# All eleven feature pairs of both SwiGLU blocks by Strassen's scheme, with three pairs' upper left quarter first

## The chip, the cores and the metric

The kernel runs on one core of one Trainium2 chip. The metric is the device time of one execution in microseconds (us). The kernel before takes 1882.31 us, the median of three runs (1882.1 to 1882.53). PE is TensorE (matrix products and transposes), DVE is VectorE, ACT is ScalarE, POOL is GpSimd, SP is SyncE, which only issues DMAs here.

## The reference, cut to what matters

One decoder layer on 1024 rows (S) of width 1024 (D): a half weighted SwiGLU, a mixing block of attention, and a second half weighted SwiGLU.

```python
def _rms(x, g):
    y = x * rsqrt(mean(x * x, axis=-1) + EPS)
    return y * g

def _swiglu(x, g, w_gate, w_up, w_down):
    h = _rms(x, g)
    return (silu(h @ w_gate) * (h @ w_up)) @ w_down

x = x + 0.5 * _swiglu(x, ffn1_norm, ffn1_w_gate, ffn1_w_up, ffn1_w_down)
h = _rms(x, mix_norm)
...                       # dilated attention and latent attention on h, giving o
x = x + o @ w_out
x = x + 0.5 * _swiglu(x, ffn2_norm, ffn2_w_gate, ffn2_w_up, ffn2_w_down)
```

The hidden width of both SwiGLUs is 2816, or 22 feature tiles of 128. The change is in the first half of a SwiGLU alone, `h @ w_gate` and `h @ w_up`, and in both SwiGLUs alike.

## The kernel before, in words

**Products.** A float32 operand is split into a rounded high part and the low rest, and a product is the sum of three matmuls, high by high (L120), high by low (L121) and low by high (L122). A matmul takes 128 contraction rows and writes 512 columns of a PSUM bank. `split` (L97) makes the parts of an operand: ACT copies the high part (L99), then DVE subtracts it from the operand to give the low part (L100).

**The two halves of h.** `ffn` (L218) normalizes the eight row tiles (`norm_rows`: squares on ACT at L186 and DVE at L183, a chain of three small steps on POOL that ends at L131, scaling on DVE at L193) into `y[0]` to `y[7]`. `bank` (L226) transposes four row tiles at one of eight column tiles into a PSUM bank. `Block.put` copies a bank out, times the gain, as a high part (ACT, L212) and a low part (DVE, L213). So h stands transposed as four Blocks of four column tiles each: B11 and B21 are rows 0 to 511 (first and second half of D), B12 and B22 are rows 512 to 1023, which need `y[4]` to `y[7]`.

**Strassen's scheme.** A pair of feature tiles, two halves of D and two halves of the rows make a product of two by two blocks. Done plainly it takes 8 block products, by Strassen's scheme (in Winograd's form) 7. One block product is four column tiles by three matmuls, 12 matmuls: a pair takes 96 per weight matrix plainly and 84 by the scheme. The scheme works on four sums of h's Blocks, T1 to T4 (`sums`, L242 to L259: T1 is B12 less B11, T2 is B22 less T1, T3 is B22 less B12, T4 is B21 less T2; made by POOL, L235 and L255, and DVE, L246, L250 and L251), and on four sums of each weight pair, S1 to S4 (`make`, L285, sums on POOL at L295). The seven products of a weight matrix are named by their weight operand: M11 with B11 and M12 with B21 give the upper left result C11 (`start`, which adds two banks, L517); S1 with T1, S3 with T3 and S2 with T2 go on from M11's bank (`middle`, L522 to L530); S4 with B22 and M22 with T4 end it (`close`, L532). `finish` (L330) multiplies the activated gate by the up result, stores the four quarters of a pair, and makes the four sums that the down projection needs, two on DVE (L347, L348) and two on POOL (L349, L350), each pair of them with a DMA behind it.

**The order of the work.** Pair 0 is done plainly: `half_unit` (L322) makes 24 matmuls for one feature tile and one row half, 8 of them in all. Feature 0's row half 0 comes first, since it needs only `y[0]` to `y[3]`; the transposes of the second row half stand behind its second unit, and the eight half units stretch over the time in which T1 to T4 are made. Pairs 1 to 10 then go by the scheme, with gate and up products interleaved; `AHEAD` products ahead the weights' sums and splits are issued (`prepare`). The loads of a weight matrix's two tiles are issued when M11 of the matrix before it is prepared. Behind pair 10 stands the down projection (L467 to L475), which is also by the scheme.

The queues are in order: each engine executes its instructions as they stand in the program, and an instruction that waits holds up all that stand behind it on that engine. A scheduler sets how the instructions of the code are interleaved per engine.

**What stands ahead of each SwiGLU.** The first one begins with loads of x from HBM: rows 0 to 3, the first tile of both weights, rows 4 to 7, the second tile of both. Ahead of the second one stands the output projection of the mixing block, a row tile at a time (`out_rows`, 24 matmuls, ended by a DVE addition at L1212); behind each row tile come its norm and the write of the tile to `x2` in HBM (POOL, L1287). All eight are done before the second SwiGLU begins.

Of the kernel before, what the change touches and what calls it, by code (L numbers as in the profile page):

```python
# [10 lines left out]
F32 = mybir.dt.float32  # L11
# [7 lines left out]
P = 128  # L19
# [28 lines left out]
EARLYH = 4  # L48
ESTEPS = 5
# [10 lines left out]
def tile_layer(ctx: ExitStack, tc: tile.TileContext, x, g1n, mixn, g2n, wg1, wu1, wd1, wg2, wu2, wd2,  # L60
# [157 lines left out]
    def ffn(rows_in, ys, gain, wg, wu, wd, act_d, xsrc, done, aside=iter(())):  # L218
# [10 lines left out]
        B11, B12, B21, B22, T1, T2, T3, T4 = (Block() for _ in range(8))  # L229

        def whole(blk, k, eng):

            d = tmp([P, 512])
            hi, lo = blk.hi_lo(k)
            eng.tensor_tensor(d, hi.bitcast(F32), lo.bitcast(F32), op=ALU.add)  # L235
            return d

        def turned(blk, th, k):
            kf = k + 4 * (blk in (B21, B22))
            blk.put(k, bank(th, kf), gcol[:, kf:kf + 1])  # L240

        def sums():  # L242
            for k in range(4):
                b12 = whole(B12, k, nc.gpsimd)
                t1 = whole(B11, k, nc.vector)
                nc.vector.tensor_tensor(t1, b12, t1, op=ALU.subtract)  # L246
                T1.put(k, t1)
                yield
                t3 = whole(B22, k, nc.gpsimd)
                nc.vector.tensor_tensor(t1, t3, t1, op=ALU.subtract)  # L250
                nc.vector.tensor_tensor(t3, t3, b12, op=ALU.subtract)  # L251
                T3.put(k, t3)
                yield
                t4 = whole(B21, k, nc.gpsimd)
                nc.gpsimd.tensor_tensor(t4, t4, t1, op=ALU.subtract)  # L255
                T2.put(k, t1)
                yield
                T4.put(k, t4)
                yield  # L259
# [7 lines left out]
        order = []  # L267
        PAIRS = range(1, NF // 2)
        for c in PAIRS:
            order += [(c, "g", w) for w in ("M11", "M12")]  # L270
            if c > 1:
                order += [(c - 1, "u", w) for w in ("S4", "M22")]
            order += [(c, "g", w) for w in ("S1", "S3", "S2")]
            order += [(c, "u", w) for w in ("M11", "M12")]
            order += [(c, "g", w) for w in ("S4", "M22")]
            order += [(c, "u", w) for w in ("S1", "S3", "S2")]
        order += [(NF // 2 - 1, "u", w) for w in ("S4", "M22")]
        raws, sums_, ready = {}, {}, {}
        made = [0]

        def load_pair(c, nme):
            if c < NF // 2:
                raws[(c, nme)] = [raw_of((wg if nme == "g" else wu)[2 * c + j]) for j in range(2)]
# [1087 lines left out]
```

## Time and profile before

| what | us |
|---|---|
| median of three runs | 1882.31 |
| the profiled execution's own time | 1881.59 |
| its span (first to last instruction) | 1879.8 |
| PE busy | 1825.7 |
| DVE busy | 1271.2 |
| ACT busy | 775.4 |
| POOL busy | 627.8 |
| first SwiGLU: PE's first transposes, and its last wait before a long stretch without waits | 7.08 and 84.00 |
| second SwiGLU's first transposes | 1221.56 |

The profile is of one execution. Its rows are of this kind: an engine, the line of the kernel, the operation, the tiles it writes and reads, how many instructions of a kind follow each other, and in brackets the idle time of the engine just before and what ended it. Matmuls are pipelined, so that the span of one (0.39 us) is longer than the distance from one to the next. The granted TensorE clock (PEclk) was 0.993 of full speed over the whole span. Outside the span lie 1881.59 - 1879.8 = 1.8 us.

### The profile page before, as it was taken

The page shows a single profiled execution, that of the slowest core. Times are in us where ns is not written, and L with a number is a line of the kernel's source. Part 1 is how long each engine was busy: PE and PEld are TensorE (multiplying, and loading weights), DVE is VectorE, ACT ScalarE, POOL GpSimd, SP SyncE. Part 2 cuts the span into 40 slices and gives each one's busy share as a digit, 9 for nine tenths or more (in the row PEclk, how much of TensorE's full clock was granted, in tenths as well). Part 3 has the DMA queues.
Part 4 walks back from the last instruction along what each step waited for, and adds up shares of the span by engine and source line. Part 5 has one row for each costly group of instructions (what it writes and reads, how often), then busy time and mean ns, then how long its engine had stood idle before and what let it go on. Part 6 is the DMA issues. An engine that isn't in the chain of part 4 may idle for free.

```text
span 1879.8 us, 25149 instructions
## 1 busy us (share of the span) xinstructions
PE 1825.7 (97%) x9088; PEld 1546.2 (82%) x9088; DVE 1271.2 (68%) x2127; ACT 775.4 (41%) x1782; POOL 627.8 (33%) x706
## 2 busy tenths in 40 slices
PE   7899999999999999999998999979999999999998
PEld 5688888888888888888998888868888888888887
DVE  7976766766968363337888683388676767678681
ACT  5333333334445242236876582243333333253550
POOL 5643455442000122332454521256445444510000
PEclk9899999999999999999999999989999999999999
DMA  4223243326943231123311232313224222397422
GB/s 179 79 90 109 95 142 122 102 78 244 343 140 107 96 128 34 34 69 112 91 37 29 57 114 78 124 56 107 96 84 135 96 99 92 105 337 269 123 62 90
DMA packets 87078, 215.50 MB, mean 115 GB/s; under 512 B 11847, under 2 KB 17689, under 8 KB 86953
## 3 DMA queue, kind: packets, MB, share of 16 engines
q1 hardware_dynamic: 69608, 154.54, 25.0%
q0 software_dynamic: 17344, 59.35, 9.3%
q8 instruction: 71, 1.16, 0.2%
q14 instruction: 55, 0.44, 0.1%
HBM read 150.32 MB, written 59.33 MB: 112 GB/s over the span
## 4 chain that ended last, share of the span: by engine, by line
PE 88%; DVE 7%; issue 2%; DMA 1%; ACT 1%; POOL 1%; SPq 0%; POOLq 0%; DVEq 0%
PE ps L122 19%; PE ps L120 19%; PE ps L121 19%; PE ps L469 7%; PE ps L468 7%; PE ps L467 7%; PE ps L781 2%; DVE slot L100 2%; PE ps L807 2%; PE ps L755 1%; PE ps L846 1%; PE ps L771 1%; PE ps L969 1%; DVE slot L213 1%; PE ps L173 1%
## 5 line engine op out<-in xcount | busy, mean ns | idle before, releaser
L120 PE MATMUL ps<-slot,slot 128*128 128x512 f32 (+3 forms) x1728 | 664.3, 386 | 8.3 <-ACT slot L358 5.4
L122 PE MATMUL ps<-slot,slot 128*128 128x512 f32 (+3 forms) x1728 | 655.2, 383 | 14.4 <-DVE slot L359 13.1
L121 PE MATMUL ps<-slot,slot 128*128 128x512 f32 (+3 forms) x1728 | 661.5, 383 | 0.0
L122 PEld LDWEIGHTS ps<-slot,slot 128*128 128x128 f32 x1728 | 326.0, 189 | 78.3 <-DVE slot L359 14.0
L120 PEld LDWEIGHTS ps<-slot,slot 128*128 128x128 f32 x1728 | 325.8, 189 | 72.8 <-ACT slot L358 6.2
L121 PEld LDWEIGHTS ps<-slot,slot 128*128 128x128 f32 x1728 | 325.9, 189 | 62.3 <-DVE slot L213 0.5
L100 DVE TENSOR_TENSOR slot<-tmp,slot 128x512 fp32r<-128x512 f32 x346 | 332.5, 963 | 61.1 <-ACT slot L99 61.1
L99 ACT ACTIVATE slot<-tmp 128x512 fp32r<-128x512 f32 x346 | 215.2, 625 | 201.9 <-PE ps L469 43.6
L100 DVE TENSOR_TENSOR slot<-slot,slot 128x512 fp32r<-128x512 f32 (+3 forms) x312 | 254.2, 825 | 25.1 <-ACT slot L99 23.7
L468 PE MATMUL ps<-slot,slot 128*128 128x512 f32 x616 | 239.9, 390 | 0.0
L469 PE MATMUL ps<-slot,slot 128*128 128x512 f32 x616 | 239.7, 389 | 0.0
L467 PE MATMUL ps<-slot,slot 128*128 128x512 f32 x616 | 237.3, 389 | 0.0
L99 ACT ACTIVATE slot<-slot 128x512 fp32r<-128x512 f32 (+3 forms) x312 | 195.5, 641 | 61.0 <-PE ps L469 39.0
L468 PEld LDWEIGHTS ps<-slot,slot 128*128 128x128 f32 x616 | 115.6, 188 | 24.1
L469 PEld LDWEIGHTS ps<-slot,slot 128*128 128x128 f32 x616 | 115.6, 188 | 24.0
L467 PEld LDWEIGHTS ps<-slot,slot 128*128 128x128 f32 x616 | 115.6, 188 | 23.8
L543 ACT ACTIVATE tmp<-tmp 128x512 f32<-128x512 f32 x80 | 50.0, 625 | 199.6 <-DVE tmp L536 108.4
L528 DVE TENSOR_TENSOR tmp<-tmp,ps 128x512 f32<-128x512 f32 x40 | 27.5, 687 | 153.3 <-ACT tmp L527 153.3
L527 ACT ACTIVATE tmp<-ps 128x512 f32<-128x512 f32 x40 | 23.9, 597 | 226.1 <-PE ps L122 226.1
L342 POOL DMA_DIRECT2D act<-slot x22 | 16.2, 734 | 252.1 <-DVE slot L339 252.1
L475 DVE SCALAR_TENSOR_TENSOR slot<-ps,slot 128x512 f32<-128x512 f32 x56 | 36.9, 685 | 79.6 <-PE ps L469 79.5
L763 ACT ACTIVATE slot<-slot,tmp 128x256 f32<-128x256 f32 (+1 forms) x128 | 59.8, 468 | 22.4 <-DVE tmp L756 21.9
(174 smaller groups left out, 2278.2 us busy)
## 6 DMA issues: line engine op xcount, KB each, us to landing
tmp<-act SPq DMA_DIRECT2D x154, 256.0 KB
act<-slot POOLq DMA_DIRECT2D x66, 512.0 KB, 4.3
slot<-in_wg_dram SPq DMA_DIRECT2D x44, 512.0 KB
slot<-in_wu_dram SPq DMA_DIRECT2D x44, 512.0 KB
slot<-in_wd_dram SPq DMA_DIRECT2D x40, 512.0 KB
slot<-in_x_dram SPq DMA_DIRECT2D x16, 512.0 KB
x_mid<-slot POOLq DMA_DIRECT2D x16, 512.0 KB, 3.0
slot<-x_mid SPq DMA_DIRECT2D x16, 512.0 KB
```

The costliest lines, as they stand in the source:

```text
L99: nc.scalar.activation(hi, src, AF.Copy)
L100: nc.vector.tensor_tensor(lo, src, hi.bitcast(F32), op=ALU.subtract)
L120: nc.tensor.matmul(pt, ah, bh, start=first and i == 0, stop=False, skip_group_check=not first)
L121: nc.tensor.matmul(pt, ah, bl, start=False, stop=False, skip_group_check=not first)
L122: nc.tensor.matmul(pt, al, bh, start=False, stop=i == total - 1, skip_group_check=not first)
L467: nc.tensor.matmul(banks[i], ah, w[:, 0, :], start=first and k == 0, stop=False, skip_group_check=not first)
L468: nc.tensor.matmul(banks[i], ah, w[:, 1, :], start=False, stop=False, skip_group_check=not first)
L469: nc.tensor.matmul(banks[i], al, w[:, 0, :], start=False, stop=k == KD - 1, skip_group_check=not first)
L543: nc.scalar.activation(q, q, AF.Silu)
L763: nc.scalar.activation(self.p[:, e, :w], self.p[:, e, :w], AF.Exp, bias=self.m[e], scale=-1.0, accum_out=self.den[e])
L781: nc.tensor.matmul(po[:, e * HD:(e + 1) * HD], self.pt[:, n * P:(n + 1) * P], self.head["values"](self.far, self.j, e, j - nb + 1), start= ...
L807: nc.tensor.matmul(pt[:, :max(w, 256)], a, b, start=i == 0, stop=i == len(mats) - 1)
```

## The change

`FRONT = 3` and `FAHEAD = 2` are new constants, `lead` is a new argument of `ffn` (0 for the first SwiGLU, 2 for the second).

- All eleven pairs go by the scheme; `unit` and `half_unit` are gone. PE has 8011 rows in the order of the program after and 8059 before: 24 matmuls fewer in each SwiGLU (8 products of 24 plainly, 14 of 12 by the scheme).
- Pairs 0, 1 and 2 (the front pairs) do C11 first. Each of gate and up has one bank: M11 goes into it, ACT copies it to the tile `p1` (L398), and M12 is added in the same bank, so that it holds C11. Later `middle` puts S2's product into a fresh bank and adds `p1` to it on DVE (L538). In the loop over the pairs, the front pairs have no M11 and M12 left, so `close_up` of the pair before stands next to S1, S3 and S2.
- `second_half` is a generator that makes the second row half: plain copies of B12 and of B21 (ACT, L242), B22 as before, and T1 to T4 on DVE straight from the transposes' banks (L259 to L275). There is no Block B12.
- The norms of `y[4 + lead]` to `y[7]` stand behind the first M11. In the second SwiGLU, `out_rows`, the norm and the write to `x2` of row tiles 6 and 7 stand there too (`last_rows`).
- All sums of weights and of activations that were on POOL (L295, L349, L350) are on DVE (L319, L366, L367). Rows of DVE: 2356 (2103 before); of POOL: 452 (692); of ACT: 1474 (1400).
- Loads: rows 4 and 5, the next weight tile, rows 6 and 7, then later weights. The front pairs' first feature tile is loaded a second time for the sums, which is 6 more loads of 512 KB in each SwiGLU.

```diff
+FRONT = 3
+FAHEAD = 2
...
-    def ffn(rows_in, ys, gain, wg, wu, wd, act_d, xsrc, done, aside=iter(())):
+    def ffn(rows_in, ys, gain, wg, wu, wd, act_d, xsrc, done, lead, aside=iter(())):
...
+        def plain(of, k, pt, kf):
+            if k % 2 == 0:
+                of.append(slot([P, 2, 512]))
+            nc.scalar.activation(of[-1][:, k % 2, :], pt, AF.Copy, scale=column(kf))
...
+        def second_half():
+            for k in range(4):
+                plain(b12, k, bank(1, k), k)
+            yield
+            banks = [bank(1, 4 + k) for k in range(4)]
+            yield
+            t1 = []
+            for k in range(4):
+                hi, lo = B11.hi_lo(k)
+                t1.append(tmp([P, 512]))
+                nc.vector.tensor_tensor(t1[k], hi.bitcast(F32), lo.bitcast(F32), op=ALU.add)
+                nc.vector.tensor_tensor(t1[k], half(b12, k), t1[k], op=ALU.subtract)
+                T1.put(k, t1[k])
+                B22.put(k, banks[k], column(4 + k))
+                t = half(b12, k)
+                nc.vector.scalar_tensor_tensor(t, banks[k], column(4 + k), t, op0=ALU.mult, op1=ALU.subtract)
+                nc.vector.scalar_tensor_tensor(t1[k], banks[k], column(4 + k), t1[k], op0=ALU.mult, op1=ALU.subtract)
+                yield
+            for k in range(4):
+                T3.put(k, half(b12, k))
+            yield
+            for k in range(4):
+                T2.put(k, t1[k])
+            yield
+            for k in range(4):
+                t = half(w21, k)
+                nc.vector.tensor_tensor(t, t, t1[k], op=ALU.subtract)
+                T4.put(k, t)
+            yield
...
-        PAIRS = range(1, NF // 2)
+        PAIRS = range(NF // 2)
+        order = [(c, m, w) for c in range(FRONT) for w in ("M11", "M12") for m in "gu"]
...
-                nc.gpsimd.tensor_tensor(src, sums_[a_] if a_ in sums_ else m[a_], sums_[b_] if b_ in sums_ else m[b_],
+                nc.vector.tensor_tensor(src, sums_[a_] if a_ in sums_ else m[a_], sums_[b_] if b_ in sums_ else m[b_],
...
-                nc.gpsimd.tensor_tensor(s43[:, 1, :], a11, a21, op=ALU.subtract)
-                nc.gpsimd.tensor_tensor(s43[:, 0, :], a12, s12[:, 1, :], op=ALU.subtract)
+                nc.vector.tensor_tensor(s43[:, 1, :], a11, a21, op=ALU.subtract)
+                nc.vector.tensor_tensor(s43[:, 0, :], a12, s12[:, 1, :], op=ALU.subtract)
...
+        for t in range(4 + lead):
             y[t] = ys(t)
+        prepare(1)
+        for k in range(4):
+            B11.put(k, bank(0, k), column(k))
+        prepare(2)
+        sums = second_half()
+        for c in range(FRONT):
+            p1[c] = slot([P, 2, 512])
+            A = [ps(), ps()]
+            for i, m in enumerate("gu"):
+                product(A[i], c, m, "M11", B11, ahead=FAHEAD)
+                nc.scalar.activation(p1[c][:, i, :], A[i], AF.Copy)
+                if c == 0 and i == 0:
+                    banks = [bank(0, 4 + k) for k in range(4)]
+                    for k in range(4):
+                        B21.put(k, banks[k], column(4 + k))
+                    for t in range(4 + lead, 8):
+                        y[t] = ys(t)
+                    for k in range(4):
+                        plain(w21, k, banks[k], 4 + k)
+                if c > 0:
+                    next(sums, None)
+            for i, m in enumerate("gu"):
+                product(A[i], c, m, "M12", B21, first=False, ahead=FAHEAD)
+                if c > 0:
+                    next(sums, None)
+            sg = tmp([P, 512])
+            nc.scalar.activation(sg, A[0], AF.Silu)
+            finish(2 * c, 0, sg, A[1])
+        for _ in sums:
+            pass
...
-            product(A, c, nme, "S2", T2, first=False)
+            if c < FRONT:
+                A = ps()
+            product(A, c, nme, "S2", T2, first=c < FRONT)
             a, q = tmp([P, 512]), tmp([P, 512])
-            nc.scalar.activation(a, A, AF.Copy)
+            if c < FRONT:
+                nc.vector.tensor_tensor(a, p1[c][:, "gu".index(nme), :], A, op=ALU.add)
+            else:
+                nc.scalar.activation(a, A, AF.Copy)
```

How the order moves on ACT at the start of the first SwiGLU, before: `slot_97` is a weight tile of the up matrix, whose split (L358) stands ahead of the squares of `y[4]` to `y[7]` (L186), the silu's table and the silu of feature 0 (L404).

```order
L358 ACTIVATE slot_250<-slot_97 128x512 [waits DMAHW6_49]
L358 ACTIVATE slot_250<-slot_97 128x512
L186 ACTIVATE slot_257,small_256<-slot_99 128x512 [waits DMAHW7_49]
L404 ACT_TABLE_LOAD
L404 ACTIVATE tmp_389<-ps_225 128x512 [waits PE_49]
L186 ACTIVATE slot_268,small_267<-slot_101 128x512 [waits DMAHW0_49]
L186 ACTIVATE slot_279,small_278<-slot_103 128x512 [waits DMAHW1_49]
L186 ACTIVATE slot_290,small_289<-slot_105 128x512 [waits DMAHW2_49]
L212 ACTIVATE slot_330<-ps_325,small_85 128x512 [waits PE_49]
```

And after, from the copy of the up matrix's M11 (L398) on: the squares are L188, the silu L414, the plain copies of B21 L242, and the last row is the split of the second half of the up matrix's first tile (`slot_101`), which the up product M12 of pair 0 multiplies.

```order
L398 ACTIVATE slot_193<-ps_195 128x512 [waits PE_49]
L188 ACTIVATE slot_245,small_244<-slot_97 128x512 [waits DMAHW6_49]
L188 ACTIVATE slot_256,small_255<-slot_99 128x512 [waits DMAHW7_49]
L414 ACT_TABLE_LOAD
L414 ACTIVATE tmp_344<-ps_194 128x512 [waits PE_49]
L188 ACTIVATE slot_267,small_266<-slot_103 128x512 [waits DMAHW1_49]
L188 ACTIVATE slot_278,small_277<-slot_105 128x512 [waits DMAHW2_49]
L242 ACTIVATE slot_288<-ps_212,small_85 128x512 [waits DVE_49]
L242 ACTIVATE slot_288<-ps_217,small_85 128x512 [waits DVE_49]
L242 ACTIVATE slot_291<-ps_222,small_85 128x512 [waits DVE_49]
L242 ACTIVATE slot_291<-ps_227,small_85 128x512 [waits DVE_49]
L101 ACTIVATE slot_294<-slot_101 128x512
```

The weight split has moved behind the silu of pair 0's gate, two of the squares and four new copies.

On DVE in the first SwiGLU, where one weight matrix is closed and the next goes on, before (in one of the first pairs; L536 and L539 are the closing additions, L100 the low parts of the next weights, L528 and L529 the additions of `middle`):

```order
L536 TENSOR_TENSOR tmp_1141<-tmp_1075,ps_1024 128x512 [waits PE_49]
L539 TENSOR_TENSOR tmp_1075<-tmp_1075,ps_1025 128x512 [waits DVE_49,PE_49]
L100 TENSOR_TENSOR slot_1165<-tmp_1163,slot_1165 128x512 [waits Activation_49]
L100 TENSOR_TENSOR slot_1180<-slot_840,slot_1180 128x512 [waits DMAHW1_49,DMASW7_49,Activation_49]
L100 TENSOR_TENSOR slot_1197<-tmp_1195,slot_1197 128x512 [waits Activation_49]
L528 TENSOR_TENSOR tmp_1213<-tmp_1212,ps_1162 128x512 [waits Activation_49]
L529 TENSOR_TENSOR tmp_1213<-tmp_1213,ps_1161 128x512 [waits DVE_49]
```

And after, in the front pairs: L549 and L552 are the closing additions of pair 0's up matrix, which wait for S4's and M22's last matmul, L319 the sums of pair 1's up weights, L538 the addition of `p1` to S2's product of pair 1's gate, L356, L364 and L366 the activations' products and sums of pair 0, the first L102 the low part of M22 of pair 1's gate, and the last row the low part of S1 of pair 1's up matrix (`slot_862`), which PE's next product needs.

```order
L549 TENSOR_TENSOR tmp_824<-tmp_800,ps_742 128x512 [waits PE_49]
L319 TENSOR_TENSOR tmp_860<-slot_746 128x512 [waits DMAHW3_49]
L319 TENSOR_TENSOR tmp_877<-slot_744,slot_746 128x512 [waits DMAHW2_49]
L356 TENSOR_TENSOR slot_826<-tmp_722,tmp_824 128x512 [waits DVE_49]
L552 TENSOR_TENSOR tmp_800<-tmp_800,ps_743 128x512 [waits PE_49]
L319 TENSOR_TENSOR tmp_895<-tmp_860,slot_744 128x512 [waits DVE_49]
L102 TENSOR_TENSOR slot_828<-slot_645,slot_828 128x512 [waits Activation_49]
L538 TENSOR_TENSOR tmp_912<-slot_348,ps_894 128x512 [waits PE_49]
L364 TENSOR_TENSOR slot_846<-slot_826,slot_346 128x512 [waits DVE_49]
L366 TENSOR_TENSOR slot_847<-slot_346,slot_826 128x512
L356 TENSOR_TENSOR slot_826<-tmp_699,tmp_800 128x512 [waits DVE_49]
L102 TENSOR_TENSOR slot_862<-tmp_860,slot_862 128x512 [waits Activation_49]
```

Ten instructions now stand between the closing addition L549 and the low part that PE's next product needs; two of the ten (L552, L538) wait for PE themselves, and the weights' sums are among them.

More of the change, by code (lines that the diff above doesn't have):

```diff
@@ L227, in bank @@
             return pt
[L229 to L242, printed above, removed]
-            for k in range(4):
[L244 to L247, printed above, removed]
-                yield
[L249 to L259, printed above, removed]
+        B11, B21, B22, T1, T2, T3, T4 = (Block() for _ in range(7))
@@ L277, in ffn, with load_units @@
         order += [(NF // 2 - 1, "u", w) for w in ("S4", "M22")]
+        units = [(True, c, m) for c in range(FRONT) for m in "gu"] + [(False, c, m) for c in PAIRS for m in "gu"]
         raws, sums_, ready = {}, {}, {}
[L279 to L283, printed above, removed]
+        made, loaded = [0], [0]
+        def load_units(n):
+            while loaded[0] < min(n, len(units)):
+                front, c, nme = u = units[loaded[0]]
+                raws[u] = [raw_of((wg if nme == "g" else wu)[2 * c + j]) for j in range(1 if front else 2)]
+                loaded[0] += 1
         def make(c, nme, which):
-            if which == "M11":
-                load_pair(*((c, "u") if nme == "g" else (c + 1, "g")))
-            f1, f2 = raws[(c, nme)]
+            front = c < FRONT and which in ("M11", "M12")
+            u = (front, c, nme)
+            load_units(units.index(u) + (3 if front else 2))
+            f1, f2 = raws[u][0], raws[u][-1]
             m = {"M11": f1[:, :512], "M12": f1[:, 512:], "M21": f2[:, :512], "M22": f2[:, 512:]}
@@ L303, in make @@
             ready[(c, nme, which)] = (s[:, 0, :], s[:, 1, :])
-            if which == "M22":
-                del raws[(c, nme)]
+            if which == "M22" or (front and which == "M12"):
+                del raws[u]
         used = [0]
@@ L319, in product @@
             products(pt, [(cut(w, k * P, (k + 1) * P), blk.hi_lo(k)) for k in range(4)], first)
-        def half_unit(w, th):
-            pt = ps()
-            lo, up = (B11, B21) if th == 0 else (B12, B22)
-            products(pt, [(cut(w, k * P, (k + 1) * P), (lo, up)[k // 4].hi_lo(k % 4)) for k in range(8)])
-            return pt
         acts = {}
@@ L409, in ffn @@
+        for _ in sums:
             pass
-        B12.t = None
+        y.clear()
         KD = NF // 2
@@ L552, in ffn @@
                 next(aside, None)
-            A, g11 = start(c, "g")
-            silu(g11)
+            A = Au = None
+            if c >= FRONT:
+                A, g11 = start(c, "g")
+                silu(g11)
             if late:
```

90 lines of the change are left out of this document (29 added, 61 removed).

## The prediction, on record before the run

> **What bounds the kernel now.** I read the page's head first, then the chain of waits, then the windows.
>
> ```profile
> span 1879.8 us, 25149 instructions
> PE 1825.7 (97%) x9088; PEld 1546.2 (82%) x9088; DVE 1271.2 (68%) x2127; ACT 775.4 (41%) x1782; POOL 627.8 (33%) x706
> PE 88%; DVE 7%; issue 2%; DMA 1%; ACT 1%; POOL 1%; SPq 0%; POOLq 0%; DVEq 0%
> ```
>
> PE makes 88% of the chain that ended last. So a matmul that goes is worth its whole time, unless PE then waits. The windows say where it waits (columns: window, length, then PE, PEld, DVE, ACT and POOL busy with their counts, granted clock, DMA share, GB/s):
>
> ```profile
> 14.00:20.00 6.00, 5.68 (x25) 4.71 (x26) 5.54 (x10) 5.98 (x12) 1.87 (x2) 1.00 0.67 255
> 40.00:60.00 20.00, 9.97 (x35) 7.42 (x34) 19.96 (x22) 7.27 (x13) 10.79 (x8) 0.74 0.15 52
> 100.00:600.00 500.00, 500.00 (x2208) 413.25 (x2207) 357.27 (x476) 186.77 (x333) 160.18 (x133) 1.00 0.43 147
> 1240.00:1280.00 40.00, 31.57 (x134) 25.40 (x133) 39.38 (x43) 15.57 (x28) 24.99 (x16) 0.87 0.10 33
> 1300.00:1800.00 500.00, 500.00 (x2208) 414.01 (x2207) 359.77 (x470) 186.09 (x333) 162.14 (x132) 1.00 0.42 142
> ```
>
> From 100 to 600 and from 1300 to 1800 PE never rests: 2208 matmuls in 500 us, **0.2265 us each**. At the start of each SwiGLU (40 to 60, 1240 to 1280) DVE is the full engine and PE starves. What PE waits for there:
>
> ```profile
> PE ps L122 <- DVE slot L359: 13.1, 2, 7.1
> PE ps L226 <- DVE slot L193: 7.3, 2, 7.1
> PE ps L120 <- ACT slot L358: 5.4, 2, 2.9
> PE ps L120 <- DVE slot L213: 1.8, 2, 1.0
> PE ps L122 <- DVE slot L100: 1.3, 1, 1.3
> PE ps L226 <- DVE slot L213: 0.9, 1, 0.9
> ```
>
> PE's own rows give place and clock (start, duration, then the idle time just before):
>
> ```profile
> 7.08 6.44 PE L226 MATMUL ps<-ident,slot 128*128 128x128 f32 x32 [7.08 <-DVE slot L193]
> 14.32 0.50 PE L120 MATMUL ps<-slot,slot 128*128 128x512 f32 x1 [0.80 <-DVE slot L213]
> 28.04 0.98 PE L226 MATMUL ps<-ident,slot 128*128 128x128 f32 x7 [0.24 <-DVE slot L193]
> 44.98 0.50 PE L120 MATMUL ps<-slot,slot 128*128 128x512 f32 x1 [2.88 <-ACT slot L358]
> 52.85 0.79 PE L122 MATMUL ps<-slot,slot 128*128 128x512 f32 x1 [7.14 <-DVE slot L359]
> ...
> 57.10 0.39 PE L120 MATMUL ps<-slot,slot 128*128 128x512 f32 x1
> 1221.56 3.65 PE L226 MATMUL ps<-ident,slot 128*128 128x128 f32 x32
> 1226.26 0.50 PE L120 MATMUL ps<-slot,slot 128*128 128x512 f32 x1 [1.04 <-DVE slot L213]
> 1254.38 0.50 PE L120 MATMUL ps<-slot,slot 128*128 128x512 f32 x1 [2.47 <-ACT slot L358]
> 1261.10 0.80 PE L122 MATMUL ps<-slot,slot 128*128 128x512 f32 x1 [5.96 <-DVE slot L359]
> ```
>
> 32 transposes take 3.65 us when nothing holds them (0.114 each) and 6.44 in the first SwiGLU, where they wait for the norms. From 52.85 to 57.10 ten matmuls take 4.25 us instead of 2.27: after a gap of 7.14 the clock is low for a while, 2.0 us lost. After 2.88 it was not.
>
> Lost before, first SwiGLU: 2.8 (slow transposes) + 0.80 + 0.24 + 0.9 + 2.88 + 7.14 + 1.3 + 2.0 = **18.1 us**. Second: 1.04 + 2.47 + 5.96, and 2.1 for the clock as in the first = **11.6**. Together 29.6 (18.06 and 11.57).
>
> **The change, part by part.**
>
> *Work removed.* 48 matmuls at 0.2265: **-10.9 us**, if PE is never made to wait more than it did. Everything else is about those 29.6 us: what takes their place. Pair 0's half units were long products with ready operands, and T1 to T4 were made beside them. Now T1 to T4 are made beside three C11, 144 matmuls, or 32.6 us, against 192 matmuls, 43.5.
>
> *Prices on DVE and ACT.* DVE is queued in order, so I walked along its order after the change with these rows:
>
> ```profile
> 13.51 5.36 DVE L213 SCALAR_TENSOR_TENSOR slot<-ps,small,slot 128x512 fp32r<-128x512 f32 x8 [0.77 <-ACT slot L212]
> 43.14 3.44 DVE L100 TENSOR_TENSOR slot<-tmp,slot 128x512 fp32r<-128x512 f32 x2
> 53.33 0.68 DVE L100 TENSOR_TENSOR slot<-tmp,slot 128x512 fp32r<-128x512 f32 x1
> 53.93 0.68 DVE L246 TENSOR_TENSOR tmp<-tmp,tmp 128x512 f32<-128x512 f32 x1
> 12.79 4.74 ACT L212 ACTIVATE slot<-ps,small 128x512 fp32r<-128x512 f32 x8 [1.93 <-PE ps L226]
> 19.20 1.28 ACT L404 ACT_TABLE_LOAD   x1
> 20.55 0.60 ACT L404 ACTIVATE tmp<-ps 128x512 f32<-128x512 f32 x1
> 21.05 0.62 ACT L186 ACTIVATE slot<-slot 128x512 f32<-128x512 f32 x1
> ```
>
> An addition in SBUF is issued every 0.60 us (53.33 to 53.93), one that reads a bank every 0.66 (5.36 for eight, less the last one's tail). Beside POOL's sums the same low part took 1.7 (3.44 for two, at 43.14). With the sums gone from POOL I take 0.60 for all; the bound on the other side is 1.7, as before. ACT's copies out of a bank take 0.59 (4.74 for eight).
>
> [...]
>
> *First SwiGLU after, in PE's order.*
> (a) The first 56 PE instructions (32 transposes, 24 of M11) wait for the same norms of `y[0]` to `y[3]`: 2.8, then 0.8, and 0.5, an estimate, for a first split that stands one step later. **4.1**, and row 57 starts at 7.08 + 3.65 + 24 x 0.2265 + 4.1 = 20.3.
> (b) The gate's M12 takes 2.7 us and some 0.4 of waits for low parts: PE is through at 23.4. Its next product needs the split of `slot_101`, which stands on ACT behind the silu, which waits for just that 23.4, then 0.60, two squares of 0.62, four plain copies of 0.59, the split's 0.53 and hand-overs of 0.5: 28.7. PE rests 5.3 us, and 0.3 more for `y[7]`: **5.6** (+0.4). The clock falls as it did after 5.96; of its 2.0 us most lies beside the wait for `y[7]`, **0.7** counts. Bound: 0 to 2.0.
> (c) At 31.6 PE has all of `y`. ACT's first copy of B12 stands behind the copy of M11 of pair 1's gate, done 20 matmuls later, at 36.1; two copies on, at 37.3, DVE can start on T1. From there to the low part of pair 0's S2 stand 54 instructions, 40 in SBUF and 14 out of banks: 24.0 + 9.2 = 33.2, with 1.2 for hand-overs 71.7. PE has 134 matmuls and 16 transposes before it needs that: 32.2, so it is there at 63.8. With 0.4 for small waits on the way: **8.3**.
> (d) Then the loop over the front pairs, which have no M11 and M12 between closing one matrix and opening the next. The closing addition L549 waits for S4's last matmul; from it to the low part of the next S1 are twelve DVE instructions, 7.4 us, while PE has 15 matmuls, 3.4. PE waits 4.0. Counted in the same way the three other closings of the front pairs give 1.5, 3.7 and 0.8: **10.0**.
> Sum 29.1, against 18.1 before.
>
> *Second SwiGLU after.* Six row tiles are out before it and two stand inside:
>
> ```profile
> 1216.32 0.69 DVE L1212 TENSOR_TENSOR slot<-ps,slot 128x512 f32<-128x512 f32 x1 [1.75 <-PE ps L122]
> 1221.76 0.69 DVE L1212 TENSOR_TENSOR slot<-ps,slot 128x512 f32<-128x512 f32 x1 [1.75 <-PE ps L122]
> ```
>
> A row tile is 5.45 us of PE work, so two of them, 10.9, cover what (a) and (b) are in the first: nothing is lost there. But `y[7]` comes later, and DVE's 54 instructions start at about 1239, with the same 32.2 of PE work beside them from about 1237: **6.5**. The loop costs a little less than in the first, since DVE has fewer rows left over: **9.0**, an estimate from (d); 0.3 for hand-overs. Sum 15.8, against 11.6.
>
> *Steady pairs.* From pair 3 on DVE has 40 instructions per pair (14 low parts, 8 weight sums, 10 additions, 8 of `finish`) at 0.63, 25 us, against 168 matmuls, 38.1. That is 66% full, and before it was 359.77 of 500, 72%. M11 and M12 stand between closing and opening again. I cost it at nothing; the cover is 3.7 us at the tightest wait that I found.
>
> *The rest at nothing.* Twelve more loads of 512 KB, on SP's queue: the share of DMA is 0.42 to 0.43; if one were late at the start, at 255 GB/s it would cost 2.1 us. Six copies L398 per SwiGLU on ACT, which has 187 of 500 us in use. POOL, past which the sums are moved, keeps the small steps of the norms, and nothing early waits for its DMAs. The middle of the program is as before.
>
> *Sum.* Lost after 29.1 + 15.8 = 44.9, before 29.6: +15.3, less 10.9: **+4.4 us**. The profiled execution took 1881.59 (its span of 1879.8 and 1.8 around it), so 1886.0; the median of the runs is 0.7 above it: **1886.7**. About 0.2% (3.8 us) is what a measurement of this kernel can tell from no change; the bounds are 1878.5 and 1886.1.
>
> **The rivals.**
>
> *R1, the front waits are half covered: faster.* The saving of 10.9 is certain, the 19 us of (d) in both SwiGLUs rest on my count of what stands between a closing and an opening. If PE had twice the cover, or DVE passed the twelve in 5.4 instead of 7.4 us, they would halve: -9.5, **1877.2**. It decides at an average of 0.45 us per instruction; no subtraction of two SBUF operands in the rows above is below 0.60. For it: DVE's total over this stretch is no more than two thirds of PE's time, so little reordering would do.
>
> *R2, the clock falls in the stretches of (c) and (d).* Before it fell only after 5.96 and 7.14. After, waits of 4 us with a few matmuls between might count as one gap: four such stretches at up to 2.0 us, less what DVE hides: +6, **1892.7**. It decides between 2.88 (kept) and 5.96 (lost), just where these waits lie. [...]
>
> *R3, the steady pairs wait too.* With the weights' sums on DVE each of the 16 steady pairs of both SwiGLUs might wait 0.5 us: +8, **1894.7**. Against it the 66%.
>
> *That the change doesn't do what it says* is excluded: the order has 48 PE rows fewer.
>
> **How the numbers follow.** Forecast 0.50 (its own spread 3.5 us to either side: within 0.2% 0.22, slower 0.28); R1 0.25 (faster 0.20, same 0.05); R2 0.18 and R3 0.07, both slower. Faster 0.20, same 0.27, slower 0.53. The range runs from just under R1, 1876, to between R2 and R3, 1894; outside are R1's lower half of 0.1 and as much of R2 and R3. The forecast's own range is 1883.2 to 1890.2.
>
> **What would show it.** Right: PE's largest waits at 23 to 29 for the ACT split L101, near 64 to 72 for L102 (S2's low part), then one of 4 us for L102 behind L549, about at 100; no waits from 160 to 640; L102 at 0.60 each. Wrong: PE without waits over 2 us after 75 (R1), a clock under 0.9 between 60 and 150 (R2), rows of waits in 200 to 600 (R3).

## The result, and the profile after

The changed kernel takes **1900.14 us** (median of 4 runs, 1898.72 to 1900.25), the kernel before 1882.42 beside it (4 runs): a ratio of **1.009, 95% interval 1.0073 to 1.0108**. Slower, as forecast, but by 17.7 us and not by 4.4, and outside the range. A second measurement of the same kernel gave 1.0079 (1.0064 to 1.0094).

The page of the kernel after, its head and the chain:

```profile
span 1898.4 us, 24982 instructions
PE 1836.4 (97%) x9040; PEld 1545.5 (81%) x9040; DVE 1239.4 (65%) x2383; ACT 787.9 (42%) x1798; POOL 273.0 (14%) x466
PE 87%; DVE 7%; ACT 3%; issue 1%; DMA 1%; POOL 0%; SPq 0%; POOLq 0%; ACTq 0%
```

Here is the puzzle in one line: PE has 48 matmuls fewer and is *busy* 10.7 us longer (1836.4 against 1825.7). More waiting would show as less busy time. PE's waits in the kernel after (total in us, times, longest):

```profile
PE ps L122 <- ACT slot L101: 17.3, 12, 5.3
PE ps L124 <- DVE slot L102: 10.7, 9, 2.2
PE ps L229 <- DVE slot L195: 9.3, 4, 7.5
```

The long waits of 7.1 and 6.0 us are gone; in their place are one of 5.3 us and many of 0.3 to 2.2 us. Stretches of the first SwiGLU after, and one of the second (columns as in the prediction: PE, PEld, DVE, ACT, POOL busy, granted clock, DMA share, GB/s):

```profile
20.00:36.00 16.00, 10.60 (x43) 8.49 (x42) 11.77 (x26) 12.11 (x24) 5.12 (x13) 0.82 0.30 110
60.00:80.00 20.00, 15.85 (x54) 11.31 (x53) 20.00 (x33) 11.54 (x22) 0.00 (x0) 0.86 0.17 53
104.00:125.00 21.00, 17.81 (x63) 13.25 (x63) 12.80 (x21) 3.67 (x6) 2.02 (x3) 0.84 0.42 138
125.00:160.00 35.00, 30.91 (x123) 23.32 (x123) 20.70 (x34) 7.79 (x13) 2.73 (x4) 0.95 0.32 113
160.00:200.00 40.00, 40.00 (x178) 33.14 (x177) 29.21 (x48) 14.64 (x26) 2.73 (x4) 1.00 0.32 111
1300.00:1330.00 30.00, 26.81 (x106) 20.73 (x105) 20.62 (x35) 7.95 (x13) 2.08 (x3) 0.90 0.21 66
```

Five of the six have a granted clock below 1.00; only from 160 on is PE full and fast. What such a place looks like on PE, at the closing of pair 0's up matrix:

```profile
107.46 0.39 PE L124 MATMUL ps<-slot,slot 128*128 128x512 f32 x1
107.92 0.50 PE L122 MATMUL ps<-slot,slot 128*128 128x512 f32 x1
...
108.96 0.39 PE L123 MATMUL ps<-slot,slot 128*128 128x512 f32 x1
110.86 0.50 PE L122 MATMUL ps<-slot,slot 128*128 128x512 f32 x1 [1.51 <-ACT slot L101]
111.20 0.40 PE L123 MATMUL ps<-slot,slot 128*128 128x512 f32 x1
113.20 0.80 PE L124 MATMUL ps<-slot,slot 128*128 128x512 f32 x1 [1.61 <-DVE slot L102]
113.80 0.63 PE L122 MATMUL ps<-slot,slot 128*128 128x512 f32 x1
...
118.49 0.56 PE L123 MATMUL ps<-slot,slot 128*128 128x512 f32 x1
118.89 0.40 PE L124 MATMUL ps<-slot,slot 128*128 128x512 f32 x1
```

From 107.46 to 113.20 are 7 matmuls, 1.59 us of work in 5.74: 4.15 us of waiting (forecast: 4.0). Then 13 matmuls take 5.69 us, 0.43 each, instead of 2.94: **2.75 us more, for the clock**. And DVE in the same time:

```profile
105.85 0.69 DVE L549 TENSOR_TENSOR tmp<-tmp,ps 128x512 f32<-128x512 f32 x1 [6.11 <-PE ps L124]
106.45 0.69 DVE L319 TENSOR_TENSOR tmp<-slot 128x512 f32<-128x512 f32 x1
...
111.86 0.69 DVE L356 TENSOR_TENSOR slot<-tmp,tmp 128x512 f32<-128x512 f32 x1
112.46 1.29 DVE L102 TENSOR_TENSOR slot<-tmp,slot 128x512 fp32r<-128x512 f32 x2
```

It waits 6.11 us for S4's end, and then does the twelve instructions of the forecast (four of the rows are shown) at 0.60 each without a gap, the last of them the low part that PE waits for.

Where the 18.6 us between the two profiled executions lie is read from PE's rows. From the start to the last matmul of the first down projection: 676.79 before, 691.12 after. From there to the first matmul of the output projection (the middle): 451.50 and 452.75. From there to the last matmul: 746.39 and 749.59. So **+14.3 in the first SwiGLU, +1.25 in the middle, +3.2 in the second**. The table has this for all kernels, as differences to the kernel before in us, each from one profiled execution; the ratio is of medians:

| kernel | ratio to before (95%) | first | middle | second |
|---|---|---|---|---|
| changed | 1.0090 (1.0073 to 1.0108) | +14.3 | +1.3 | +3.2 |
| changed, again (after2) | 1.0079 (1.0064 to 1.0094) | +14.1 | +1.1 | +3.3 |
| fill | 1.0008 (0.9998 to 1.0017) | +8.9 | -3.5 | -0.5 |
| fill_half | 1.0043 (1.0028 to 1.0058) | +8.9 | +1.1 | -0.3 |
| ahead8 | 1.0017 (1.0007 to 1.0026) | +6.5 | +0.6 | -2.6 |
| fahead3 | 1.0068 (1.0051 to 1.0084) | +7.8 | +0.7 | +6.8 |
| front1 | 1.0032 (1.0017 to 1.0046) | +7.7 | 0.0 | -1.5 |
| sums_pool | 0.9973 (0.9963 to 0.9984) | +4.3 | -2.5 | -4.8 |
| front_pool | 0.9941 (0.9925 to 0.9957) | +2.2 | -4.0 | -8.1 |
| old_dve | 0.9992 (0.9983 to 1.0002) | -0.1 | +2.7 | -0.2 |
| pool_f3 | 0.9983 (0.9974 to 0.9993) | +4.8 | -0.4 | -5.6 |
| pool_f3_a8 | 0.9916 (0.9899 to 0.9934) | -0.8 | +0.8 | -12.4 |
| best | 0.9884 (0.9869 to 0.9898) | -6.3 | +3.0 | -15.0 |

### The profile page after: what moved, and what is told of

The parts are those of the page before. It is cut to its first block, busy times and chain, and to the rows that moved or that the text cites. A ratio compares the mean times of both kernels' runs of the same rounds, so it can differ in the third digit from the quotient of the medians.

```text
span 1898.4 us, 24982 instructions
## 1 busy us (share of the span) xinstructions
PE 1836.4 (97%) x9040; PEld 1545.5 (81%) x9040; DVE 1239.4 (65%) x2383; ACT 787.9 (42%) x1798; POOL 273.0 (14%) x466
## 4 chain that ended last, share of the span: by engine, by line
PE 87%; DVE 7%; ACT 3%; issue 1%; DMA 1%; POOL 0%; SPq 0%; POOLq 0%; ACTq 0%
PE ps L124 19%; PE ps L122 18%; PE ps L123 18%; PE ps L476 7%; PE ps L477 7%; PE ps L475 7%; PE ps L798 2%; DVE slot L102 2%; PE ps L824 1%; PE ps L772 1%; PE ps L863 1%; PE ps L788 1%; DVE tmp L319 1%; ACT slot L101 1%; PE ps L986 1%
## 5 line engine op out<-in xcount | busy, mean ns | idle before, releaser
L124 PE MATMUL ps<-slot,slot 128*128 128x512 f32 (+3 forms) x1712 | 648.5, 387 | 10.8 <-DVE slot L102 10.7
L102 DVE TENSOR_TENSOR slot<-slot,slot 128x512 fp32r<-128x512 f32 (+3 forms) x340 | 238.3, 712 | 31.8 <-ACT slot L101 30.3
L102 DVE TENSOR_TENSOR slot<-tmp,slot 128x512 fp32r<-128x512 f32 x346 | 236.9, 691 | 27.8 <-ACT slot L101 23.9
L101 ACT ACTIVATE slot<-slot 128x512 fp32r<-128x512 f32 (+3 forms) x340 | 213.3, 642 | 84.3 <-PE ps L477 43.1
L549 DVE TENSOR_TENSOR tmp<-tmp,ps 128x512 f32<-128x512 f32 x44 | 30.3, 688 | 172.4 <-PE ps L124 172.4
L540 ACT ACTIVATE tmp<-ps 128x512 f32<-128x512 f32 x32 | 19.2, 598 | 155.7 <-PE ps L124 155.7
L541 DVE TENSOR_TENSOR tmp<-tmp,ps 128x512 f32<-128x512 f32 x44 | 30.2, 687 | 79.1 <-ACT tmp L540 79.0
```

What stands on the lines that cost most here:

```text
L101: nc.scalar.activation(hi, src, AF.Copy)
L102: nc.vector.tensor_tensor(lo, src, hi.bitcast(F32), op=ALU.subtract)
L124: nc.tensor.matmul(pt, al, bh, start=False, stop=i == total - 1, skip_group_check=not first)
L549: nc.vector.tensor_tensor(q, a, Dk, op=ALU.add)
```

## The experiments

The theory after the traces: the front pairs' waits are as forecast, made by what stands behind a closing addition on DVE, and most of them cost the clock besides. The rivals: that the slow matmuls are slow for another reason; that DVE has simply too much to do; that the missing M11 and M12 are the cause, whoever makes the sums.

**fill: is it idle time that slows the matmuls?** Zero weights, so that nothing is added to a sum:

```diff
+            for _ in range(fill if i == 0 else 0):
+                nc.tensor.matmul(pt, zero, bh, start=False, stop=False, skip_group_check=not first)
...
+            fill = {"S1": 9, "S3": 7}.get(which, 0) if (c, nme) in ((1, "u"), (2, "u")) else 0
```

> The changed kernel with 16 more matmuls at each of four places (nine behind the first two matmuls of S1, seven behind those of S3, for the up matrices of pairs 1 and 2 in both SwiGLUs). Their weight operand is a tile of zeros, so they add nothing to the sums; they stand where TensorE waits for DVE's low part of S1. Theory A (the front waits are as long as I forecast, but each is followed by 2 us or more of low clock, because TensorE is idle there): 64 matmuls more, 14.5 us of TensorE work, lie in waits that are there anyway; the matmuls behind them run at 0.227 us instead of 0.43, 1.6 to 2.6 us less at each place, and the whole is 6 to 9 us faster than the changed kernel, about 1892 us. Theory B (the matmuls are slow there for another reason, such as DVE reading and writing the same memories at its full rate): they stay slow, and the time is 1899 to 1904.

The same place with 16 matmuls more:

```profile
108.56 2.23 PE L129 MATMUL ps<-slot,zero 128*128 128x512 f32 x9
...
111.09 1.77 PE L129 MATMUL ps<-slot,zero 128*128 128x512 f32 x7
...
113.28 0.50 PE L130 MATMUL ps<-slot,slot 128*128 128x512 f32 x1
113.62 0.39 PE L126 MATMUL ps<-slot,slot 128*128 128x512 f32 x1
```

And the stretch around it, as a window:

```profile
104.00:125.00 21.00, 20.93 (x92) 16.68 (x91) 14.80 (x25) 5.10 (x9) 2.02 (x3) 1.00 0.43 139
```

PE goes on at 113.28, as at 113.20 without them, and then at full pace; the clock of the stretch is 1.00 instead of 0.84. The two SwiGLUs gain 5.5 and 3.7 us, **9.2 together**, by 64 matmuls *more*: theory A's mechanism, just above its 6 to 9. At the four places together the clock had cost 9.75 us (2.75 and 1.7 in the first SwiGLU, 2.6 and 2.7 in the second). DVE does the same twelve instructions behind its closing addition at the same 0.60 us each, so theory B is out. The profiled execution is 14.0 us shorter in all; the other 4.8 are in the middle, of which below, and so the 1885.4 us of the whole lie below the 1892 that theory A named.

**fill_half: how much idle time does it take?** The edit is `{"S1": 4, "S3": 3}`.

> As in the run with 16 zero matmuls at each of four places, but with 7 (four behind S1's first two matmuls, three behind those of S3): 1.6 us of the 4.4 that TensorE is idle there are filled, 2.8 stay idle. Theory A (the clock falls when idle time adds up to more than about 3 us of some 6, in one piece or in several): the clock stays up at the four places and the SwiGLUs take the same time as with 16, within 1.5 us. Theory B (it falls whenever matmuls come in small groups, or the fill works only because nothing idle is left): the matmuls behind run at 0.43 us again, and the SwiGLUs take 6 to 9 us more than with 16.

```profile
107.30 1.08 PE L129 MATMUL ps<-slot,zero 128*128 128x512 f32 x4
...
112.02 0.50 PE L130 MATMUL ps<-slot,slot 128*128 128x512 f32 x1 [1.60 <-DVE slot L106]
112.36 0.40 PE L126 MATMUL ps<-slot,slot 128*128 128x512 f32 x1
```

The wait of 1.60 us ahead of the low part is there again, and the clock stays up all the same; both SwiGLUs take what they took with 16 (within 0.3 us). That is theory A in this: not one gap decided here but what several of them added up to. Its 3 us of some 6 no run shows as the limit; what the rows show in its place is in the account of the clock below, by which this place was close.

**ahead8: is it the order of DVE's work?**

```diff
-AHEAD = 5
+AHEAD = 8
```

> The changed kernel with AHEAD = 8 instead of 5: the weights' sums and splits are issued eight products ahead, so that S1, S3 and S2 of the next matrix stand ahead of the closing additions on DVE and not behind them. Theory A (waits in the front pairs come from what stands behind a closing addition on DVE, and the clock falls with them): of the four waits of the loop in each SwiGLU about three go, with the low clock behind them; 10 to 14 us in the first SwiGLU and as much as 10 in the second are to be had, and the time is 1876 to 1886. Theory B (DVE has simply too much work over the whole front stretch): the order of its work doesn't matter, the waits move to another product, and the time is within 4 us of 1900. Theory C (tiles run out with three more products made ahead): new waits in the steady pairs too, 1900 or more.

The waits of the same stretch shrink to one, on PE and in the window:

```profile
114.34 0.50 PE L124 MATMUL ps<-slot,slot 128*128 128x512 f32 x1 [0.98 <-DVE slot L102]
```

```profile
104.00:125.00 21.00, 20.02 (x89) 16.22 (x88) 14.24 (x24) 5.03 (x9) 2.03 (x3) 1.00 0.42 146
```

7.8 us less in the first SwiGLU and 5.8 in the second, and DVE does the same work. The time, 1886.5, is half a microsecond above the top of theory A's range: the order counts, but waits of 0.9 to 1.1 us are still left in the loop of the first SwiGLU, one of 2.6 us in that of the second, and the gap of 4.7 us at 31 too.

**sums_pool: all sums back on GpSimd.**

```diff
-                nc.vector.tensor_tensor(src, sums_[a_] if a_ in sums_ else m[a_], sums_[b_] if b_ in sums_ else m[b_],
+                nc.gpsimd.tensor_tensor(src, sums_[a_] if a_ in sums_ else m[a_], sums_[b_] if b_ in sums_ else m[b_],
...
-                nc.vector.tensor_tensor(s43[:, 1, :], a11, a21, op=ALU.subtract)
-                nc.vector.tensor_tensor(s43[:, 0, :], a12, s12[:, 1, :], op=ALU.subtract)
+                nc.gpsimd.tensor_tensor(s43[:, 1, :], a11, a21, op=ALU.subtract)
+                nc.gpsimd.tensor_tensor(s43[:, 0, :], a12, s12[:, 1, :], op=ALU.subtract)
```

> The changed kernel with the weights' sums and the two activation sums back on GpSimd; all else as changed. Theory A (sums on DVE stand in the way between closing one matrix and opening the next): the waits of the front loop shrink from 10 us to about 2 in the first SwiGLU and the low clock goes with them, less what DVE loses beside GpSimd (1.7 instead of 0.6 us for an operation): 1884 to 1892. Theory B (the front pairs without M11 and M12 between closing and opening are the cause, whoever makes the sums): within 3 us of 1900. Theory C (DVE is slower beside GpSimd by more than the sums that it is spared): above 1903.

1878.3 us, 0.9973: below theory A's range, and **faster than the kernel before**. 10.1 us of the gain are in the first SwiGLU, 8.0 in the second, 3.8 in the middle. Theory A's 8 to 16 us less than the changed kernel was too low. Against the kernel before the two SwiGLUs are only 0.5 us shorter together (+4.3 and -4.8), and the 2.5 us in the middle make most of its lead. So the rest of the change, Strassen for pair 0 and C11 first, comes out even here, and the sums on DVE, where they stood, were the loss. The stretch from 104 to 125:

```profile
104.00:125.00 21.00, 20.67 (x90) 16.35 (x90) 18.73 (x22) 7.44 (x13) 11.61 (x10) 1.00 0.48 162
```

22 DVE instructions are 18.73 us busy here, 0.85 each beside GpSimd's work, against 21 in 12.80 before the edit, 0.61 each: DVE is slower and PE waits less.

**front_pool: which of the sums?** `(nc.gpsimd if c < FRONT else nc.vector).tensor_tensor(src, ...)`; the activations' sums stay on DVE.

> The changed kernel with the weights' sums of pairs 0, 1 and 2 alone on GpSimd; all other sums stay on DVE. Theory A (only the sums in the front pairs stand in PE's way): the same time as with all sums on GpSimd, 0.997 to 1.000 of the kernel before. Theory B (sums of the steady pairs or of the activations matter as well): between that and the changed kernel, 1.003 to 1.007.

0.9941: better than with all sums on GpSimd, past theory A's range on the fast side. The weights' sums of three pairs carry the whole loss; the other sums (the weights' of the steady pairs and the activations') do better on DVE, by 2.1 and 3.4 us in the two SwiGLUs. Which of these two kinds was not tried.

**old_dve: the same sums on DVE in the kernel before.** Its L295, L349 and L350 with `nc.vector`, and nothing else.

> The kernel before with one edit: the weights' sums and the two activation sums on DVE instead of GpSimd; pair 0 plainly, T1 to T4 as before. Theory A (sums on DVE hurt only where a matrix closes and the next opens with no M11 and M12 between): this kernel has no such place, so it moves little, within 4 us of the kernel before. Theory B (the sums on DVE cost by themselves, in the steady pairs too): 8 to 20 us slower than the kernel before, waits of PE spread over 160 to 460.

0.9992 (0.9983 to 1.0002), and the SwiGLUs within 0.3 us. Theory A: where M11 and M12 stand between closing and opening, the sums on DVE cost nothing. From 80 on PE has no wait:

```profile
80.00:104.00 24.00, 24.00 (x108) 19.87 (x107) 16.25 (x27) 8.14 (x15) 1.43 (x2) 1.00 0.30 110
104.00:125.00 21.00, 21.00 (x94) 17.41 (x93) 11.76 (x20) 7.21 (x13) 0.72 (x1) 1.00 0.22 76
```

So neither half of the change does the harm alone: sums on DVE are free in the old order, and with the sums on GpSimd the SwiGLUs of the new order take no longer than those of the old (0.5 us less).

**front1: one front pair instead of three.** `FRONT = 1`, sums on DVE.

> The changed kernel with FRONT = 1: pair 0 alone does C11 first, and from pair 1 on M11 and M12 stand between closing one matrix and opening the next; all sums stay on DVE. Theory A (the sums on DVE hurt where a matrix closes and the next opens without M11 and M12 between): no such waits after T1 to T4 are made, but only 48 matmuls instead of 144 beside making them, so the wait there grows from 6 to 15 us or more in each SwiGLU: 1895 to 1912. Theory B (DVE is overloaded in the front whatever stands between): waits of 2 us go on behind 100, and with the longer wait the time is above 1912. Theory C (too little is left of C11 to matter, and the loop was the loss): 1880 to 1890.

1889.7, at the top of theory C's range. In the first SwiGLU no wait is left behind 62:

```profile
36.00:60.00 24.00, 15.27 (x48) 9.59 (x46) 23.11 (x38) 14.23 (x25) 0.00 (x0) 0.71 0.17 58
104.00:125.00 21.00, 21.00 (x95) 17.38 (x94) 12.97 (x21) 7.45 (x14) 0.72 (x1) 1.00 0.30 116
```

But PE is busy only 15.27 of 24 us, at a clock of 0.71, while T1 to T4 are made: with 48 matmuls of C11 instead of 144 the wait there is larger, as theory A had it, though by less than it said: 9.4 us of idle time from 36 to 62, where the changed kernel has 4.9 from 36 to 80. So the number is theory C's, and both mechanisms show.

**fahead3: the gap at 31.** `FAHEAD = 3`.

> The changed kernel with FAHEAD = 3 instead of 2: the split of the up matrix's second half is issued one product earlier, ahead of the silu, the squares and the copies on ACT. Theory A (the gap of 5.3 us at 25.4 is made by what stands ahead of that split on ACT, and it costs 2.2 us of clock as well): the first SwiGLU gains 5 to 8 us, the second at most 1, 1892 to 1896. Theory B (DVE's chain that makes T1 to T4 is what bounds the front stretch, and it starts no sooner): the wait goes, but comes back later in the same stretch; 1897 to 1901.

The first SwiGLU gains 6.5 us (theory A), the second loses 3.6, which neither theory had. There is no such gap there to close, and from 1270 to 1370 the matmuls come in small groups at clocks of 0.89 to 0.94 in three windows. The whole takes 1896.98 us.

**pool_f3: both.** `ahead=FAHEAD + (lead == 0)`, so for the first SwiGLU alone, on top of sums_pool.

> The changed kernel with all sums on GpSimd, and FAHEAD = 3 in the first SwiGLU alone. What is left in the first SwiGLU with the sums on GpSimd is a gap of 4.7 us at 31.4 with the low clock behind it. Theory A (that gap is ACT's order, and independent of the sums): 4 to 7 us less than with the sums on GpSimd alone, 0.994 to 0.995 of the kernel before. Theory B (DVE's chain for T1 to T4 bounds the stretch): 0.996 to 0.998.

0.9983, so theory A falls for this kernel, and theory B's 0.996 to 0.998 is missed by a hair: the gap at 31 is gone, and the first SwiGLU is no faster (+0.5 us), since a wait for DVE came in its place 48 us later:

```profile
79.47 0.80 PE L124 MATMUL ps<-slot,slot 128*128 128x512 f32 x1 [4.68 <-DVE slot L102]
```

With the sums on GpSimd DVE's own chain for T1 to T4 bounds this stretch (20.00 of 20 us busy from 60 to 80).

**pool_f3_a8:** the one before with `AHEAD = 8`.

> The one before with AHEAD = 8 as well. The waits that are left in the loop of the front pairs are under 2 us each, some 5 us in each SwiGLU. If they are still DVE's order, up to 4 us less in each, 0.990 to 0.993 of the kernel before; if GpSimd's sums of 1.3 us each, or the tiles that run out, bound it, nothing or more time, 0.994 to 0.998.

1868.48, 0.9916, inside the first range, and 5.6 and 6.7 us in the two SwiGLUs where I had up to 4. That fits DVE's order as what was left; the wait of 4.68 us at 79.47 has become one of 1.93 at 75.60.

**after2: the changed kernel again.**

> The changed kernel once more, word for word. The middle part of the program, whose instructions the change leaves in place, took 447.5 to 454.2 us in the profiles so far; the slowdown of 17.7 us had 1.25 of it. If that scatter is of the execution, the middle is somewhere else this time and the ratio to the kernel before stays at 1.007 to 1.011; the two SwiGLUs again take 14 and 3 us more than before, within 1 us.

The SwiGLUs repeat to 0.3 us, and so does the middle, 452.62 against 452.75. So what I took for a scatter of the execution, 447.5 to 454.5 us over the kernels, is none: it belongs to the kernel. The order of the program shows why that can be: changed kernel and fill_half have the same order on DVE in the middle and take 452.75 and 452.62 there; in fill the six instructions of a rotary step (L1035 to L1040 of the changed kernel) stand further ahead, and it takes 447.98. The waits for that step, in the changed kernel and in fill:

```profile
PE ps L986 <- DVE tmp L1040: 6.4, 4, 2.7
```

```profile
PE ps L993 <- DVE tmp L1047: 2.9, 3, 1.6
```

The scheduler sets this order by what went before. That order and not something else makes the difference was not tried by itself; the granted clock differs there as well, low for 10.2 us of the middle in the changed kernel and for 3.4 in fill.

**best:** weights' sums of the front pairs on GpSimd, all others on DVE, `AHEAD = 8`, `FAHEAD = 3` in the first SwiGLU.

> The changed kernel with the weights' sums of the three front pairs on GpSimd and all others on DVE, AHEAD = 8, and FAHEAD = 3 in the first SwiGLU. Theory A (the front pairs' waits were the whole loss, and the steady pairs have room on DVE): the two short waits per SwiGLU that were left with all sums on GpSimd (for a bank that DVE releases late) go too, 0.988 to 0.992 of the kernel before, at or below the best so far (0.9916). Theory B (eight products ahead and DVE's sums don't go together): 0.994 or more.

1861.82 us (4 runs, 1860.69 to 1863.08), **0.9884 (0.9869 to 0.9898)**, 21.7 us less than the kernel before in the same session and 38 less than the changed one. The longest of PE's waits behind the transposes of the first SwiGLU:

```profile
58.24 0.50 PE L122 MATMUL ps<-slot,slot 128*128 128x512 f32 x1 [2.15 <-ACT slot L398]
...
75.45 0.50 PE L124 MATMUL ps<-slot,slot 128*128 128x512 f32 x1 [1.96 <-DVE slot L102]
```

And behind them PE is full:

```profile
80.00:104.00 24.00, 24.00 (x108) 19.87 (x107) 17.34 (x24) 6.92 (x12) 10.62 (x10) 1.00 0.21 78
125.00:160.00 35.00, 35.00 (x156) 29.00 (x155) 20.84 (x35) 9.40 (x16) 3.10 (x5) 1.00 0.33 113
```

Its middle is the slowest of them all, 454.45; with the 447.5 of front_pool it would be some 7 us faster still, which no run tried.

## Why the prediction was wrong, point by point

- **The matmuls saved, -10.9.** Right: 48 PE rows fewer. The two SwiGLUs of best are 21.3 us shorter than before, which by this count are these 10.9 and a third of the 29.6 that the kernel before lost.
- **DVE's and ACT's prices.** Right: 0.60 us for an instruction in SBUF, the twelve behind L549 in one run, and four copies of ACT in 2.41 us at 28.09. (ACT has 16 ACTIVATE rows more than before in the profile, 1474 and 1458, and not 74 more.)
- **The waits of the first SwiGLU.** Nearly right in sum. Forecast and measured times of PE's landmarks: gate's M12 done 23.4 and 25.8; gap behind it 5.3 and 5.30, to 28.7 and 31.07; the first product with a low part after it 31.6 and 36.21; low part of S2 71.7 and 77.17. Of the 5.5 us by which the last is late 2.4 arise at the start and some 2.2 in the slow clock behind the gap. The start was misread: the 6.44 us of the 32 transposes before are no wait for the norms, since the row at 7.08 has no gap inside it: the first two dozen stand 0.21 us apart and the last ones 0.11, and the sixteen at 32.94 in the kernel after, at a granted clock of 0.50, stand 0.21 us apart too. After the change the first transposes are as slow (1.12 us for four) and wait for the norms besides, 0.81, 0.81 and 0.28 us. Of the 8.3 us of (c) some 7 came, not as one wait but in pieces of at most 1.7 us. Then the closings: 4.0, 1.5 and 3.7 forecast, 4.15, 1.64 and 3.93 in PE's rows; the fourth, 0.8, doesn't show.
- **The step that failed: the clock.** In (b) I put 0.7 us for it, and none in (c) and (d), which is the term that the sum lacked: I took the length of one idle gap for what the clock goes by ("It decides between 2.88 (kept) and 5.96 (lost)", in R2). Behind 31.07 it cost 2.4, behind 63.92 and 77.17 1.7 each, behind 113.20 2.75, behind 148.88 1.7: **10.3 us** in the first SwiGLU; behind 1289.52, 1325.32 and 1359.25 1.7, 2.6 and 2.7: **7.0** in the second. That is 16.6 us more than forecast. The second SwiGLU lost 20.2 in all (11.6 before, 5.4 of saved matmuls, 3.2 slower), so 13.2 in waits, 2.6 less than I had; the first's waits were 0.9 less; the middle 1.25 more. That makes about 14.4, and the profiled time was 14.2 above the forecast.
- **What the clock went by in these traces.** Even the kernel before doesn't bear out the reading of 2.88 and 5.96. The rows below have the granted clock in it around the gaps of the first SwiGLU (two rows) and behind the gap of 2.47 us in the second (one row), then around 112 us in the kernel after (two rows) and in fill_half (one row). The columns are as above; PE's busy time counts the spans of the matmuls, which are longer than their 0.2265 us.

```profile
43.22:46.63 3.41, 0.73 (x2) 0.30 (x2) 3.41 (x3) 2.67 (x5) 3.41 (x3) 1.00 0.70 270
46.63:56.87 10.24, 4.02 (x10) 3.15 (x11) 10.24 (x12) 3.97 (x7) 4.42 (x3) 0.50 0.00 0
1254.95:1265.19 10.24, 4.28 (x11) 3.23 (x11) 10.24 (x13) 3.72 (x7) 4.34 (x3) 0.50 0.01 4
108.60:112.01 3.41, 1.49 (x5) 0.59 (x4) 3.41 (x7) 0.63 (x1) 0.00 (x0) 1.00 0.01 4
112.01:118.83 6.82, 5.63 (x13) 4.46 (x14) 6.19 (x11) 1.53 (x3) 1.87 (x3) 0.50 0.35 94
109.75:113.16 3.41, 1.80 (x7) 1.19 (x8) 3.41 (x7) 0.00 (x0) 0.58 (x1) 1.00 0.10 37
```

The clock fell at 1254.95, just behind the gap of 2.47 us, when that of 5.96 (1255.14 to 1261.10 by the rows) had hardly begun, so that its length can't have decided. At 46.63 it fell about 1 us into the gap of 7.14, with 1.8 of the 2.88 us in the 3.41 us ahead. In all fourteen traces the stretches of low clock inside the program last 3.41 us or a multiple of it (6.83, 10.24, 13.65, 20.48), and in one trace all their starts and ends lie whole multiples of 3.41 us apart. Divide both SwiGLUs of all fourteen traces (17 to 650 and 1240 to 1780 us) into pieces on that grid, count 0.2265 us of work for a matmul, and leave out the pieces with transposes and those in which the clock was low. After all 52 pieces with up to 1.29 us of work the clock fell, and after none of the 4561 with more than 1.41. Three lie between: 1.31 (ahead8) and 1.40 (fill_half, 109.75 to 113.16) kept it, 1.40 (front1) lost it. The piece from 108.60 to 112.01 in the kernel after has 0.91.

A piece of 3.41 us at low clock cost 1.7 us, the size of most of the losses above: from 77.17 to 81.39 in the kernel after eleven matmuls take 4.22 us instead of 2.49. The same kernel need not lose the same in every execution: of the four of after2 one took 1895.30 us at a mean clock of 0.991, the others 1899.24 to 1900.55 at 0.985 to 0.987.

- **R2 was the case** and had 0.18. Its place and mechanism were right; its price of 6 us, "four such stretches at up to 2.0 us, less what DVE hides", was too small: there were eight, at 1.7 to 2.75, and DVE hides next to nothing of it, as fill shows, which got 9.2 back of the 9.75 at its four places. The gaps of 1.51 and 1.61 us here are both shorter than the 2.88 that was taken as kept, and with 0.91 us of work in their piece the clock was lost.
- **R1** (waits half covered) is not what happened, though what it looked at, little reordering, is what ahead8 did by design. **R3** is refuted: no wait from 160 to 640, and none from 1370 to 1780.
- **"The middle of the program is as before"** was wrong by 1.25 us: the instructions are the same, their order on DVE is not.
- **The sums on DVE.** I costed them there at 0.60 us, since beside POOL's sums a low part had taken 1.7 (the row at 43.14), and followed that row, by which leaving them on GpSimd would bring nothing back. Putting them on GpSimd for the front pairs alone brought 12.1 and 11.3 us. Beside GpSimd an instruction on DVE is dearer (from 104 to 125 in front_pool 24 of them are busy for 19.50 us, 0.81 each), and yet PE's waits there shrink to 0.83 and 0.41 us, since the sums no longer stand in the way. The prices were right; what failed is the step from them to the view that GpSimd would bring nothing, since the place of the sums in DVE's queue decided, and not DVE's total.

## What to carry to other kernels

Count a wait of TensorE not by itself: where small groups of matmuls left up to 1.29 us of work in 3.41, the slow matmuls behind cost 1.7 to 2.75 us more in the kernel after, and filling the idle time with matmuls that change nothing paid (9.2 us in fill). Ask what stands between the instruction that waits and the one that is waited for. DVE took its instructions in the order of the program: in the kernel after the loads of pair 1's up weights (issued by 83.30) had landed by 88.6, but the sums of them (L319) began at 106.45, behind the 6.11 us for which L549 waited. A sum of 0.60 us put there cost more than one of 1.47 to 1.50 us on GpSimd (means of L295 in the kernel before). A step that is free in one order (the sums on DVE, 0.9992 in old_dve) cost 23 us of the two SwiGLUs in another (front_pool against the changed kernel).

## What the runs showed of the hardware

- **The clock.** In these traces it went by the work in pieces of 3.41 us, not by the length of one gap: it fell after every piece with up to 1.29 us of matmuls and after none with more than 1.41 (both SwiGLUs of all fourteen traces, without transposes). So it stayed up through a gap of 2.10 us (sums_pool, ending at 55.64) and through 2.57 us idle in 5.74 (fill_half, 106.28 to 112.02). It fell with 4.15 us idle in the same 5.74 (the kernel after, two gaps of 1.51 and 1.61 among the pieces), and with 3.1 idle in 4.3 (72.90 to 77.17, no gap over 1.68). A low clock lasted 3.41 us or a multiple of it, with a matmul every 0.43 us.
- **Matmuls with zero weights counted as work** for the clock: with 16 of them from 104 to 125 in fill it stayed at 1.00, without them it was 0.84.
- **DVE beside GpSimd.** In the front stretch of sums_pool an instruction on DVE took 0.85 us on average instead of 0.61 (18.73 us for 22 and 12.80 for 21, from 104 to 125), and the two SwiGLUs were 18 us shorter all the same.
